# Weighted sum of two expert outputs: the order of three small transfers on ScalarE's queue

## The chip, the cores and the metric

The kernel runs on one core of a Trainium2 chip. The metric is the device time of the kernel in microseconds (us), the median of several runs. Its work is done by VectorE (DVE in the profile) and ScalarE (ACT); SyncE (SP) issues DMAs, and so does ScalarE. Sixteen DMA engines move the data between the chip's main memory (DRAM) and the on-chip buffer, which has 128 partitions.

## The reference

```python
def setup_inputs():
    batch, seq, hidden, n_experts, k = 16, 1024, 512, 8, 2
    return {
        "expert_outputs": np.random.randn(batch, seq, k, hidden).astype(np.float32),
        "combine_weights": np.random.randn(batch, seq, k).astype(np.float32),
    }

def reference(expert_outputs, combine_weights):
    weights = combine_weights[..., np.newaxis]
    return np.sum(expert_outputs * weights, axis=2).astype(np.float32)
```

For each of 16 x 1024 = 16,384 tokens, two rows of 512 numbers are multiplied by a weight each and added. 67 MB are read and 34 MB written.

## The kernel before

The 16,384 tokens are laid over 128 partitions, 128 tokens (`per`) on each. The last 13 (`LAST`) of each partition are a block of their own in DRAM, so the tokens of a partition are `main` = 115 and then 13. The 128 tokens are cut into ten tiles (`TILES`) of 12 or 13 tokens a partition. A tile has about 6.5 MB of input, and the on-chip buffer `et` has four rooms (`ROOM`), so the first four tiles are loaded at the start and a later tile is loaded into a room once the store of what was in it is done.

**Loads** are issued by SP (`load`, L76). The first four tiles take five loads (`FIRST`): 2 tokens a partition (1024 KB, cut to rows of 4,096 bytes), 11 (5632 KB, one row of 45,056 bytes a partition), 13, 12 and 13. They are called the first to the fifth load here. The first tile is the first and the second load together.

**Work on a tile** (`combine`): for eight of the ten tiles VectorE multiplies the whole tile by the broadcast weights (L88) and adds the halves (L97). In one tile ScalarE does part of the multiplying (L92 beside L94 and L96), and the last tile goes token by token through ScalarE and VectorE (L102, L103).

**Stores** (L130) are issued by ScalarE's queue, the last two by SP's.

**The weights** lie in `wt`, with the view `wk`. They come in three transfers on ScalarE's queue: the main weights, for the first 115 tokens of each partition (`weights(nc.scalar, 0, main)`, issued at L79; 128 rows of 920 bytes), and the last weights, for the other 13, in two halves of 64 partitions (L114; rows of 104 bytes).

**The zeroes**: VectorE fills `zt`, 16 x 128, with zeroes (L108), and one transfer (L111) writes them to 16 places of the output, 512 bytes at each, at the head of each sixteenth of the main block. The stores later write these places again, so the first store waits for the zeroes to land. The result does not depend on them.

The order on each engine is the order of the program text (`tc.manual_schedule()`). The built program hands out eight completion counters to the DMAs, in turn, in the order of the text. The ninth DMA of the text is the fifth load, and it has the counter of the first one; SP therefore waits, before it issues the fifth load, until the DMA that comes first in the text has landed.

Of the kernel before, what the change touches and what calls it, by code (L numbers as in the profile page):

```python
# [1 line left out]

# [4 lines left out]


@with_exitstack
def kernel(  # L10
    ctx: ExitStack,
    tc: tile.TileContext,
    expert_outputs: bass.AP,
    combine_weights: bass.AP,
    out: bass.AP,
):

    nc = tc.nc
    b, s, k, h = expert_outputs.shape
    assert k == 2
    n = b * s
    P = nc.NUM_PARTITIONS
    per = n // P
    assert per * P == n

    ROOM = [13, 13, 12, 13]
    ROOMS = len(ROOM)  # L30
    SITE = [sum(ROOM[:i]) for i in range(ROOMS)]
    TILES = [13, 13, 12, 13, 13, 13, 12, 13, 13, 13]
    FIRST = [2, 11, 13, 12, 13]
    STORES = [[0], [1], [2], [3], [4], [5], [6], [7, 8], [9]]
    WHOLE = [0, 1, 2, 3, 4, 5, 6, 7]
    MIXED = [8]
    ALONE = 3
    FREE = {9: 0}
    LAST = 13
    assert all(c <= ROOM[g % ROOMS] for g, c in enumerate(TILES))  # L40
    assert sum(TILES) == per and [g for st in STORES for g in st] == list(range(len(TILES)))
    main = per - LAST
    starts = [sum(TILES[:g]) for g in range(len(TILES))]

    def rows(x):

        first = x[0 : P * main, :].rearrange("(p t) f -> p t f", p=P)
        second = x[P * main : n, :].rearrange("(p t) f -> p t f", p=P)
        return lambda t, c: first[:, t : t + c, :] if t < main else second[:, t - main : t - main + c, :]

    flat = out.rearrange("b s h -> (b s) h")
    eo = rows(expert_outputs.rearrange("b s k h -> (b s) (k h)"))
    cw = rows(combine_weights.rearrange("b s k -> (b s) k"))
    o = rows(flat)

    dt = mybir.dt.float32
    mult = mybir.AluOpType.mult
    add = mybir.AluOpType.add
    copy = mybir.ActivationFunctionType.Copy

    pool = ctx.enter_context(tc.tile_pool(name="all", bufs=1))
    et = pool.tile([P, sum(ROOM), k * h], dt)
    halves = et.rearrange("p j (k h) -> p (j k) h", k=k)
    wt = pool.tile([P, per * k], dt)
    wk = wt.rearrange("p (t k) -> p t k", k=k)
    zt = pool.tile([16, 128], dt)
    warm = pool.tile([P, 1], dt)

    def place(t):
        g = max(g for g in range(len(TILES)) if starts[g] <= t)  # L70
        return SITE[g % ROOMS] + t - starts[g]

    def load(t, c, **kw):
        at = place(t)
        assert place(t + c - 1) == at + c - 1
        nc.sync.dma_start(out=et[:, at : at + c], in_=eo(t, c), **kw)  # L76

    def weights(q, t, c):
        q.dma_start(out=wk[:, t : t + c, :], in_=cw(t, c))  # L79

    def combine(g, base):
        at, c, t0 = SITE[g % ROOMS], TILES[g], starts[g]
        if g in WHOLE or g in MIXED:
            room = halves[:, k * at : k * (at + c), :]
            x0, x1 = et[:, at : at + c, 0:h], et[:, at : at + c, h : 2 * h]
            if g in WHOLE:
                wb = wt[:, k * t0 : k * (t0 + c)].unsqueeze(2).to_broadcast([P, k * c, h])
                nc.vector.tensor_tensor(out=room, in0=room, in1=wb, op=mult)  # L88
            else:
                for i in range(ALONE, c):  # L90
                    x = et[:, at + i, 0:h]
                    nc.scalar.activation(out=x, in_=x, func=copy, scale=wt[:, k * (t0 + i) : k * (t0 + i) + 1])  # L92
                w1 = wk[:, t0 : t0 + c, 1:2].to_broadcast([P, c, h])
                nc.vector.tensor_tensor(out=x1, in0=x1, in1=w1, op=mult)  # L94
                w0 = wk[:, t0 : t0 + ALONE, 0:1].to_broadcast([P, ALONE, h])
                nc.vector.tensor_tensor(out=x0[:, 0:ALONE], in0=x0[:, 0:ALONE], in1=w0, op=mult)  # L96
            nc.vector.tensor_tensor(out=halves[:, base : base + c, :], in0=x0, in1=x1, op=add)  # L97
            return
        for i in range(c):
            t = k * (t0 + i)  # L100
            x0, x1 = halves[:, k * (at + i), :], halves[:, k * (at + i) + 1, :]
            nc.scalar.activation(out=x0, in_=x0, func=copy, scale=wt[:, t : t + 1])  # L102
            nc.vector.scalar_tensor_tensor(  # L103
                out=halves[:, base + i, :], in0=x1, scalar=wt[:, t + 1 : t + 2], in1=x0, op0=mult, op1=add
            )

    with tc.manual_schedule():
        nc.vector.memset(zt, 0.0)  # L108

        ahead = flat[0 : P * main, :].rearrange("(q t) h -> q (t h)", q=16)  # L110
        nc.scalar.dma_start(out=ahead[:, 0:128], in_=zt)  # L111
        weights(nc.scalar, 0, main)
        for half in (slice(0, P // 2), slice(P // 2, P)):
            nc.scalar.dma_start(out=wk[half, main:per, :], in_=cw(main, per - main)[half])  # L114
        nc.scalar.activation(out=warm, in_=nc.const_aps.tensor(1.0, (P, 1), dt), func=copy)  # L115

        t = 0
        for i, c in enumerate(FIRST):
            load(t, c, **({"max_dma_last_dim": k * h * 4} if i == 0 else {}))
            t += c  # L120
        assert t == sum(TILES[:ROOMS])
        for j, st in enumerate(STORES):
            room = FREE.get(st[0], st[0] % ROOMS)
            base, c = SITE[room] * k, 0
            for g in st:
                combine(g, base + c)
                c += TILES[g]
            assert c <= k * ROOM[room]
            q = nc.sync if j in (7, 8) else nc.scalar
            q.dma_start(out=o(starts[st[0]], c), in_=halves[:, base : base + c, :])  # L130
            for g in st:
                if g + ROOMS < len(TILES):
                    load(starts[g + ROOMS], TILES[g + ROOMS])


# [1 line left out]
_INS = ['expert_outputs', 'combine_weights']  # L137
_OUTS = [((16, 1024, 512), 'float32')]


# [23 lines left out]
```

## Time and profile before

| | |
|---|---|
| time, median of 3 runs | 238.95 us (238.85 to 239.05) |
| span of the profiled execution | 237.1 us |
| outside the span, by the median | 1.85 us |
| VectorE busy | 190.0 us (80%) |
| ScalarE busy | 15.8 us (7%) |
| moved by DMA | 100.80 MB, mean 425 GB/s |

The span is that of one execution, taken by the hardware profiler, from the first instruction to the last. The times were taken without it, and the difference is taken as the same for both kernels. In the profile's rows L76 is line 76 of the kernel; SPq and ACTq are the queues of SP and ScalarE; `x <- y` gives what is written and what is read, or who waited for whom. q1 is the DMA queue that SP issues to, q10 that of ScalarE.

### The profile page before, as it was taken

The numbers are of one execution on the slowest core, as the hardware profiler recorded it, in microseconds if no ns is written. First come the engines' busy times: TensorE is split into PE (matmuls) and PEld (weight loads), VectorE is DVE, ScalarE is ACT, GpSimd is POOL, SyncE is SP. The second block draws the span as 40 slices with busy tenths as digits, with TensorE's granted clock in tenths as the row PEclk, the third lists the DMA queues.
The fourth block names the chain that finished last, engine by engine and source line by source line (L and its number), as shares of the span: only waits on it lengthen the run. The fifth ranks groups of instructions, "written<-read, shape, count | busy, mean of one in ns | idle before, by whom it ended". The sixth has DMA issues, their size and how long they took to land.

```text
span 237.1 us, 154 instructions
## 1 busy us (share of the span) xinstructions
DVE 190.0 (80%) x33; ACT 15.8 (7%) x25; POOL 0.2 (0%) x4
## 2 busy tenths in 40 slices
DVE  0006999999999999999999998998499969919400
ACT  2000000000000000000000000000000055019200
POOL 0000000000000000000000000000000000000000
DMA  8999999989999999999899999999899999899996
GB/s 300 388 481 434 432 421 398 470 348 485 449 431 458 431 440 390 486 420 420 359 492 409 409 509 392 431 503 431 359 431 503 420 397 483 381 431 431 431 431 287
DMA packets 3344, 100.80 MB, mean 425 GB/s; under 512 B 512, under 2 KB 656, under 8 KB 912
## 3 DMA queue, kind: packets, MB, share of 16 engines
q1 hardware_dynamic: 2000, 77.33, 75.9%
q10 hardware_dynamic: 1344, 23.47, 23.0%
HBM read 67.24 MB, written 33.56 MB: 425 GB/s over the span
## 4 chain that ended last, share of the span: by engine, by line
DVE 55%; DMA 36%; issue 1%; ACT 0%; DVEq 0%; ACTq 0%; SPq 0%
DVE et L88 35%; DVE et L97 17%; DMA out_dram<-et 17%; DMA et<-in_expert_outputs_dram 12%; DMA wt<-in_combine_weights_dram 8%; DVE et L103 3%; ACT et L102 0%; DVEq L159 0%; ACTq L111 0%; DVE zt L108 0%; DVEq L88 0%; SPq L76 0%; ACTq L102 0%
## 5 line engine op out<-in xcount | busy, mean ns | idle before, releaser
L88 DVE TENSOR_TENSOR et<-et,wt 128x13312 f32<-128x13312 f32 (+1 forms) x8 | 110.0, 13754 | 23.8 <-DMA wt<-in_combine_weights_dram 18.7
L97 DVE TENSOR_TENSOR et<-et 128x6656 f32<-128x6656 f32 (+1 forms) x9 | 62.8, 6973 | 0.4
L92 ACT ACTIVATE et<-et,wt 128x512 f32<-128x512 f32 x10 | 6.2, 708 | 188.0 <-DMA et<-in_expert_outputs_dram 188.0
L103 DVE SCALAR_TENSOR_TENSOR et<-et,wt 128x512 f32<-128x512 f32 x13 | 8.7, 747 | 5.0 <-ACT et L102 5.0
L102 ACT ACTIVATE et<-et,wt 128x512 f32<-128x512 f32 x13 | 8.1, 707 | 14.0 <-DMA et<-in_expert_outputs_dram 14.0
L94 DVE TENSOR_TENSOR et<-et,wt 128x6656 f32<-128x6656 f32 x1 | 7.1, 7093 | 2.3 <-DMA et<-in_expert_outputs_dram 2.3
L96 DVE TENSOR_TENSOR et<-et,wt 128x1536 f32<-128x1536 f32 x1 | 1.8, 1751 | 0.0
L115 ACT ACT_TABLE_LOAD x1 | 1.3, 1283 | 3.1 <-issue 3.1
L108 DVE MEMSET zt<- 16x128 f32 x1 | 0.2, 165 | 0.8 <-PEq L148 0.8
L115 ACT ACTIVATE warm<-const-float32-1.0 128x1 f32<-128x1 f32 x1 | 0.2, 203 | 0.0
L148 POOL MEMSET const-bfloat16-1.0<- 128x1 bf16 x1 | 0.1, 102 | 0.0
L148 POOL MEMSET const-uint8-127<- 128x1 uint8 x1 | 0.1, 101 | 0.0
L148 POOL MEMSET const-float32-0.0<- 128x1 f32 x1 | 0.1, 99 | 0.2 <-issue 0.2
L148 POOL MEMSET const-float32-1.0<- 128x1 f32 x1 | 0.1, 98 | 0.0
## 6 DMA issues: line engine op xcount, KB each, us to landing
et<-in_expert_outputs_dram SPq DMA_DIRECT2D x7, 6656.0 KB, 32.2
out_dram<-et ACTq DMA_DIRECT2D x5, 3328.0 KB, 34.7
et<-in_expert_outputs_dram SPq DMA_DIRECT2D x2, 6144.0 KB, 41.1
out_dram<-et SPq DMA_DIRECT2D x1, 6656.0 KB, 19.9
out_dram<-et ACTq DMA_DIRECT2D x2, 3072.0 KB, 37.2
et<-in_expert_outputs_dram SPq DMA_DIRECT2D x1, 5632.0 KB, 18.2
out_dram<-et SPq DMA_DIRECT2D x1, 3328.0 KB, 14.0
et<-in_expert_outputs_dram SPq DMA_DIRECT2D x1, 1024.0 KB, 5.0
```

The lines of the kernel that those rows point to most:

```text
L88: nc.vector.tensor_tensor(out=room, in0=room, in1=wb, op=mult)
L92: nc.scalar.activation(out=x, in_=x, func=copy, scale=wt[:, k * (t0 + i) : k * (t0 + i) + 1])
L94: nc.vector.tensor_tensor(out=x1, in0=x1, in1=w1, op=mult)
L96: nc.vector.tensor_tensor(out=x0[:, 0:ALONE], in0=x0[:, 0:ALONE], in1=w0, op=mult)
L97: nc.vector.tensor_tensor(out=halves[:, base : base + c, :], in0=x0, in1=x1, op=add)
L102: nc.scalar.activation(out=x0, in_=x0, func=copy, scale=wt[:, t : t + 1])
L103: nc.vector.scalar_tensor_tensor(out=halves[:, base + i, :], in0=x1, scalar=wt[:, t + 1 : t + 2], in1=x0, op0=mult, op1=add)
L108: nc.vector.memset(zt, 0.0)
L115: nc.scalar.activation(out=warm, in_=nc.const_aps.tensor(1.0, (P, 1), dt), func=copy)
L148: nc = _bacc.Bacc("TRN2", target_bir_lowering=False, num_devices=1)
```

## The change

ScalarE's queue issues the main weights first, then the zeroes, then the two halves of the last weights. Before, it was the zeroes, the main weights, the two halves. Nothing is added or taken away.

```diff
     with tc.manual_schedule():
         nc.vector.memset(zt, 0.0)
 
+        weights(nc.scalar, 0, main)
         ahead = flat[0 : P * main, :].rearrange("(q t) h -> q (t h)", q=16)
         nc.scalar.dma_start(out=ahead[:, 0:128], in_=zt)
-        weights(nc.scalar, 0, main)
         for half in (slice(0, P // 2), slice(P // 2, P)):
             nc.scalar.dma_start(out=wk[half, main:per, :], in_=cw(main, per - main)[half])
```

In the built program three more things differ. The zeroes are the second DMA of the text and have the second counter, and the main weights have the first. The fifth load thus waits for the main weights to land, where it waited for the zeroes. The first multiply (L88) and the first store (L130) wait for the same transfers as before, under the other counters.

## The prediction

> **What bounds the kernel now.** I read the page's slices and queues first, since this kernel does little but move bytes.
>
> ```profile
> span 237.1 us, 154 instructions
> DVE 190.0 (80%) x33; ACT 15.8 (7%) x25; POOL 0.2 (0%) x4
> ...
> DMA  8999999989999999999899999999899999899996
> ...
> DMA packets 3344, 100.80 MB, mean 425 GB/s; under 512 B 512, under 2 KB 656, under 8 KB 912
> ...
> q1 hardware_dynamic: 2000, 77.33, 75.9%
> q10 hardware_dynamic: 1344, 23.47, 23.0%
> ```
>
> VectorE is busy 80% of the span, but the two queues (q1 is SP's, q10 ScalarE's) keep the 16 DMA engines busy for 75.9 + 23.0 = 98.9% of it. Next I cut the span into stretches, to see whether the engines ever run dry. The columns are the stretch, its length, the busy time of DVE, ACT and POOL, the clock, the DMA share and GB/s. A packet counts where it starts, so a share can pass 1.
>
> ```profile
> 0.00:1.80 1.80, 0.17 (x1) 0.00 (x0) 0.20 (x4) 1.00 0.00 0
> 1.80:2.80 1.00, 0.00 (x0) 0.00 (x0) 0.00 (x0) 1.00 0.98 131
> 2.80:4.00 1.20, 0.00 (x0) 0.91 (x1) 0.00 (x0) 1.00 0.96 386
> ...
> 20.00:60.00 40.00, 39.93 (x4) 0.00 (x0) 0.00 (x0) 1.00 1.02 435
> 60.00:100.00 40.00, 39.93 (x5) 0.00 (x0) 0.00 (x0) 1.00 0.98 423
> 100.00:145.00 45.00, 44.52 (x5) 0.00 (x0) 0.00 (x0) 1.00 1.01 436
> 145.00:184.00 39.00, 34.31 (x4) 0.00 (x0) 0.00 (x0) 1.00 1.02 441
> 184.00:213.00 29.00, 22.18 (x4) 6.43 (x11) 0.00 (x0) 1.00 1.00 432
> ```
>
> From 2.8 us on the DMA share is about 1 in every stretch, at 423 to 441 GB/s. So from there the end is set by bytes, and the change moves no byte in or out. Only the first 2.8 us have room: nothing for 1.8 us, then 1 us with busy engines that move only 131 GB/s. The chain of waits tells another story, and I hold it against this one:
>
> ```profile
> 1.01 0.39 ACTq L111
> 1.40 0.03 issue
> 1.43 18.21 DMA wt<-in_combine_weights_dram
> ...
> 19.73 14.04 DVE et L88
> ...
> 33.78 7.09 DVE et L97
> ```
>
> By the chain the main weights, issued at 1.43 and landed at 1.43 + 18.21 = 19.64, release the first multiply (L88) at 19.73. The 20:60 and 60:100 rows above then show VectorE busy 39.93 of 40 us in both, so the chain says that an earlier start is worth having. The DMA shares say that VectorE and the DMA engines are both full there, and that the bytes decide the end. I go by the bytes.
>
> The three timed runs have a median of 238.95, which is 1.85 over the profiled span. I keep that 1.85 and sum against 237.1.
>
> **Part 1: the zeroes' memset no longer stands ahead of the main weights.** These are the issues at the start (start, length), then the transfers by size in KB and median us from issue to landing:
>
> ```profile
> 0.73 0.44 SPq L76 DMA_DIRECT2D et<-in_expert_outputs_dram  x1
> 1.01 0.39 ACTq L111 DMA_DIRECT2D out_dram<-zt  x1
> 1.22 0.46 SPq L76 DMA_DIRECT2D et<-in_expert_outputs_dram  x1
> ...
> et<-in_expert_outputs_dram SPq DMA_DIRECT2D x1, 5632.0 KB, 18.2
> et<-in_expert_outputs_dram SPq DMA_DIRECT2D x1, 1024.0 KB, 5.0
> out_dram<-zt ACTq DMA_DIRECT2D x1, 8.0 KB, 3.9
> ```
>
> The zeroes wait for the memset on VectorE (L108) and are issued at 1.01. The weights wait for nothing, so they can be issued about when SP issues its first load, 0.73: that is 1.43 - 0.73 = 0.7 us earlier. They are worth more than 0.7 at the landing, because of what they queue beside:
>
> ```profile
> q1 hardware_dynamic: 133, 0.54, 51.8%
> ...
> q10 hardware_dynamic: 32, 0.01, 2.8%
> ...
> q1 hardware_dynamic: 144, 5.90, 101.7%
> q10 hardware_dynamic: 144, 0.12, 2.6%
> ...
> q10 hardware_dynamic: 80, 0.01, 0.6%
> ```
>
> The first row is the stretch 0:3.9, in which q1 alone moved packets (133). The second is 3.9:5.2: q10's 32 are the zeroes, 16 packets and 16 completions. The next two are 6.6:20, where 144 packets of q1 stand against 144 of q10 (the 128 weight rows and 16 completions): they take turns, one for one, and each weight row waits out a 45,056-byte row of the second load. On an engine that is (20 - 6.6) / 8 = 1.7 us for each of its 8 weight rows, and this is why 115 KB need 18 us. The last row is 20:30, the last weights (64 of their 128 rows there).
>
> If the weights take the place of the zeroes, their first rows come at about 4 us, while the first load still has 256 - 133 = 123 rows of 4 KB to go, near 8 on each engine. The weights' 8 rows for each engine take turns with these, and land at 5 to 6 us; if two or three of them slip behind into the second load, each costs 1.7 us, and the landing is at about 10. Either way it is ahead of the second load, issued at 1.22 and landed 18.2 later, at 19.42. That load then releases the multiply. The gain at the multiply is at most 19.64 - 19.42 = 0.22 us, less what the zeroes and the last weights now put in front of the second load's end: 0.7 + 0.6 = under 1.3% of stretches of 5 to 10 us, some 0.1 us (taking half of the 2.8% of 1.3 us for the zeroes gives 0.02, twice the 0.6% of 10 us for the last weights gives 0.12). So VectorE starts some 0.1 us earlier. By the shares of about 1 from 20 us on, that is worth nothing at the end; if this cover were gone and VectorE alone set the end, it would be worth that 0.1.
>
> **Part 2: the zeroes move behind the weights, on ScalarE's queue alone.** Their 16 rows then land with or soon after the main weights, at 6 to 21 us instead of 1.01 + 3.9 = 4.9. They move past no other queue, but two waits follow them. The first store (L130) rewrites those places, so it waits for them; it is issued when the first sum is done, and the first multiply and sum need 14.04 and 7.09 us from 19.73, so at about 40.9. The other wait is SP's, for the fifth load:
>
> ```profile
> SPq L76 <- DMA out_dram<-zt: 2.1, 1, 2.1
> ...
> 4.92 0.33 SPq L76 DMA_DIRECT2D et<-in_expert_outputs_dram  x1
> ...
> et<-in_expert_outputs_dram SPq DMA_DIRECT2D x1, 6144.0 KB, 50.9
> ```
>
> The fifth load shares a completion counter with whatever ScalarE issues first. Now it waits 2.1 us for the zeroes and goes at 4.92. After the change it waits for the main weights, so it goes at 6 to 10, at the worst at 19.6. Queued behind it on SP is the sixth load, which needs a finished store anyway. SP's ring holds the fourth load (6144 KB) until over 50 us, so the fifth has over 30 us of slack. I cost this at nothing; the cover is those three loads already in the ring, and if they had landed by 19.6, each us of wait would be a us of idle DMA.
>
> **Part 3: two queues issue at once at the start.** This is the only term that can move the end.
>
> ```profile
> L76 SPq DMA_DIRECT2D et<-in_expert_outputs_dram x11: 327/328/643, 0.7 to 183.9; - x11
> ```
>
> An issue of SP's takes 328 ns alone, and up to 643 at the start where ScalarE issues beside it (0.44 and 0.46 above). In the kernel before SP's first issue has 1.01 - 0.73 = 0.28 us to itself; after, it hasn't. The bound above is 0.643 - 0.328 = +0.32 us on the first load. The bound below: weight rows that run while the engines only move 131 GB/s cost nothing there, and are gone from the full stretch later, 2.6% of 13.4 us = -0.35. I take 0, the middle, since nothing says which is nearer.
>
> A third price is between: if SP's first issue has to wait until ScalarE's is through, it loses one such issue, by the zeroes' row 0.39 us, and the time is 239.3 to 239.4. The bound from 0.643 speaks for something like it. By the Trainium skill (Perfetto Trace Analysis, DMA Instruction — HWDGE) the generator of DMA descriptors is shared by issuing queues and locked for exclusive use while it works for one, which would make that the price whenever ScalarE comes first; the trace, where the issues of both queues lengthen beside each other but overlap, agrees only in part.
>
> **The sum:** 237.1 + 0 (bytes) + 0 (start of VectorE, covered) + 0 (fifth load, covered) + 0 (-0.35 to +0.32, the start) + 1.85 = 238.95, say 239.0, with a range of its own of 238.6 to 239.3. A measurement of this kernel tells no change from about 0.2%, 0.48 us, so this is "same".
>
> **Rivals.**
> - *Slower: the weights get in front of the first load.* The zeroes came second, 0.28 after the load's issue, and showed no packet before 3.9, over 2.9 us after their own issue at 1.01; the first load's packets began 1.8 - 0.73 = 1.07 after its issue. So being second cost at least 1.8 us behind 256 rows. If the weights win the race at 0.73, the first load is second behind 128 rows: half of that, 0.9 us, in which the weights' own 0.35 us of work gets done: +0.55 to +0.9, 239.5 to 239.85, I say 239.6. If the 1 us of 131 GB/s repeats for the first load as well, it is +1.0. It decides as soon as ScalarE's first issue starts no later than SP's. For it: both would start at about 0.73, and the weights are a simpler pattern. Against it: the load may still go first, and then its packets run on as before.
> - *Faster: the chain is right.* The weight rows fall into the slow start, so the second load, no longer taking turns with them, lands 0.35 us earlier, at 19.07. VectorE then starts 19.64 - 19.07 = 0.57 earlier and, being busy 39.93 of 40, carries it to the end: 238.4. Against it: the weights' first rows may come as late as the zeroes', at 4 us, when the engines are already full.
> - *The change doesn't do what it says.* The weights' first rows still come after 5 us and take turns with the second load; they land near 19.5, the zeroes and the fifth load go behind them, and the time stays at 239.0.
>
> **The numbers.** The forecast has 0.40, the change without effect 0.08, the wait for one whole issue (239.3 to 239.4) 0.06; all three are "same", 0.54. The slower rival has 0.31, the faster one 0.15. The point is the likeliest case, 239.0. The range takes in the faster rival's 238.4 and the slower one's 239.85: 238.4 to 239.9.
>
> **What would show it.** In the changed profile the main weights should land at 5 to 10 us, and the idle time ahead of the first multiply should name the second load, ending at 19.5 to 19.7. SP's wait for the zeroes should be one for the main weights. The rows from 2.8 us on should keep a share of 1. The slower rival shows as a first load that lands later than 0.73 + 5.0, with few GB/s between 1.8 and 4; the faster one as a multiply that starts by 19.2 with a span shorter by as much. I am wrong if the engines run dry anywhere after 5 us, or if the end moves by more than the first 5 us do.

## The result, and the profile after

The changed kernel takes 239.5 us (median of 22 runs, 238.83 to 241.06), the kernel before 238.9 (22 runs, 238.83 to 240.95). The ratio is 1.0021, with a 95% interval of 1.0012 to 1.0031: slower by about 0.2%, 0.6 us by the medians. More telling than the median is the spread. Most runs of the kernel before lie within 0.3 us. Those of the changed kernel fall into groups: four at 238.83 to 238.90, as before, four at 239.05 to 239.15, eleven at 239.45 to 239.73, three at 240.0 and above.

The profiled run took 238.84, so it belongs to the first group and shows no loss. Span and queues, of the page after:

```profile
span 237.1 us, 154 instructions
...
q1 hardware_dynamic: 2000, 77.33, 75.7%
q10 hardware_dynamic: 1344, 23.47, 23.2%
```

The issues at the start of the changed kernel, from its timeline:

```profile
0.73 0.43 ACTq L79 DMA_DIRECT2D wt<-in_combine_weights_dram  x1
0.73 0.44 SPq L76 DMA_DIRECT2D et<-in_expert_outputs_dram  x1
```

Both queues issue at 0.73, as foretold. The transfers (KB, us from issue to landing):

```profile
et<-in_expert_outputs_dram SPq DMA_DIRECT2D x1, 5632.0 KB, 18.2
et<-in_expert_outputs_dram SPq DMA_DIRECT2D x1, 1024.0 KB, 5.3
wt<-in_combine_weights_dram ACTq DMA_DIRECT2D x1, 115.0 KB, 3.4
...
out_dram<-zt ACTq DMA_DIRECT2D x1, 8.0 KB, 6.4
```

The main weights land at 0.73 + 3.4 = 4.1 us instead of 19.64. The first load takes 5.3 instead of 5.0. The chain of waits and SP's waits:

```profile
1.22 18.22 DMA et<-in_expert_outputs_dram
...
19.57 14.04 DVE et L88
...
144.46 39.34 DMA out_dram<-et
```

```profile
SPq L76 <- DMA et<-in_expert_outputs_dram: 3.2, 1, 3.2
```

The second load has taken the weights' place ahead of the first multiply, which starts at 19.57 instead of 19.73. The last of these lines corrects a statement made ahead of the result: the fifth load does not wait for the main weights here but for the first load (3.2 us, then issued at 6.07). In the built program it is the first load that has the same counter as the fifth, and not the transfer that comes first in the text.

### The profile page after: what moved, and what is told of

It is laid out like the page before. It is cut to its first block, busy times and chain, and to the rows that moved or that the text cites. A ratio compares the mean times of both kernels' runs of the same rounds, so it can differ in the third digit from the quotient of the medians.

```text
span 237.1 us, 154 instructions
## 1 busy us (share of the span) xinstructions
DVE 190.0 (80%) x33; ACT 15.8 (7%) x25; POOL 0.2 (0%) x4
## 4 chain that ended last, share of the span: by engine, by line
DVE 55%; DMA 36%; issue 1%; ACT 0%; DVEq 0%; SPq 0%; ACTq 0%
DVE et L88 35%; DMA et<-in_expert_outputs_dram 20%; DVE et L97 17%; DMA out_dram<-et 17%; DVE et L103 3%; ACT et L102 0%; DVEq L159 0%; SPq L76 0%; DVEq L88 0%; ACTq L102 0%
## 5 line engine op out<-in xcount | busy, mean ns | idle before, releaser
L88 DVE TENSOR_TENSOR et<-et,wt 128x13312 f32<-128x13312 f32 (+1 forms) x8 | 110.0, 13754 | 23.7 <-DMA et<-in_expert_outputs_dram 23.7
L115 ACT ACTIVATE warm<-const-float32-1.0 128x1 f32<-128x1 f32 x1 | 0.2, 204 | 0.0
```

## The experiments

The times of the kernel before on the same chips were 238.87 to 238.88 (medians).

**The changed kernel again.** No edit; the aim is a profile of a run that lost time.

> The changed kernel once more, unaltered. Its 22 runs lay at 238.83 to 241.06 with a median of 239.5, and the one that was profiled took 238.84, so the profile in hand shows a run without the loss. Theory A (a race: both queues issue at 0.73, and the loss comes from how the two sets of descriptors fall at the start): the times spread again over more than 0.5, from 238.8 up, and a profile of a run above 239.3 shows the loss inside the first 20 us, as a first or second load that lands 0.3 to 1 us later. Theory B (a fixed cost of small weight rows ahead of the first load): the times gather near one value, 239.5. Theory C (the order that is set up at the start is carried on, and the time goes later, where a store and a load take turns): the first 20 us look alike, and a row of the DMA share well below 1 stands somewhere after 20 us.

239.49 (11 runs, 238.81 to 239.74), ratio 1.0021 (1.0012 to 1.0030). The profiled run took 239.37. Two more runs were profiled, with these expectations:

> The changed kernel once more, for one more profile beside the two in hand. In the one of 238.84, ScalarE's queue (q10) moved 86 packets in the first 2.8 us and SP's (q1) 23; in the one of 239.37 it was 5 against 32. Theory A: the two go together. With over 50 packets of q10 in the first 2.8 us the time is 238.8 to 239.1; with under 20 it is 239.3 to 239.8, and the first load's landing is over 5.5 us from its issue. Theory B (weight rows ahead cost): the other way round. No link: either count with either time.

> As for the run before: the changed kernel, a fourth profile, and the same link of packet count and time by theory A (over 50 packets of q10 by 2.8 us with 238.8 to 239.1, under 20 with 239.3 to 239.8).

They took 238.85 and 239.52. So there are four profiles of one program, two without the loss and two with it. What each queue moved in the first 2.8 us (packets, MB, share) tells them apart. First the run of 238.84, then that of 238.85:

```profile
q10 hardware_dynamic: 86, 0.08, 19.2%
q1 hardware_dynamic: 23, 0.09, 13.4%
```

```profile
q10 hardware_dynamic: 97, 0.09, 18.0%
q1 hardware_dynamic: 31, 0.13, 17.7%
```

And the two that lost time, of 239.37 and of 239.52:

```profile
q1 hardware_dynamic: 32, 0.13, 33.6%
q10 hardware_dynamic: 5, 0.00, 0.6%
```

```profile
q1 hardware_dynamic: 41, 0.17, 31.9%
q10 hardware_dynamic: 14, 0.01, 1.4%
```

In the runs without loss most of the 128 weight rows go in the slow first us. In the others the first load's rows go first, and most of the weight rows come among them after 2.8 us. In all four the first issues of the two queues start within 0.01 us of each other, so these do not show what decides. Theory A's link was drawn from the first two profiles; the other two bear it out.

Where the time goes can be read from the loads' landings. First and fourth load of the run of 239.52, then of the run of 238.85 (the fourth is issued at about 2.2 in both):

```profile
et<-in_expert_outputs_dram SPq DMA_DIRECT2D x1, 1024.0 KB, 5.6
...
et<-in_expert_outputs_dram SPq DMA_DIRECT2D x1, 6144.0 KB, 51.3
```

```profile
et<-in_expert_outputs_dram SPq DMA_DIRECT2D x1, 1024.0 KB, 5.2
...
et<-in_expert_outputs_dram SPq DMA_DIRECT2D x1, 6144.0 KB, 50.8
```

The first load lands 0.4 us later and the fourth, at 53 us, 0.5; the difference at the end is 0.67. A landing is that of the slowest of 16 DMA engines, and the packet records show that it is the slowest that fell back: in the run of 239.37 the third load lands on the 16 engines from 34.84 to 35.51 us, in the kernel before from 34.85 to 35.24. The first engine is as early, the last 0.27 later. These are the packets that start after 235 us, for the runs of 238.84, 239.37 and 239.52 (16 of them are the last store's completions):

```profile
DMA packets 16, 0.00 MB, mean 0 GB/s; under 512 B 16, under 2 KB 16, under 8 KB 16
```

```profile
DMA packets 23, 0.19 MB, mean 37 GB/s; under 512 B 16, under 2 KB 16, under 8 KB 16
```

```profile
DMA packets 27, 0.29 MB, mean 59 GB/s; under 512 B 16, under 2 KB 16, under 8 KB 16
```

In the runs with the loss 7 and 11 rows have yet to start, in the run without it none. A second part is lost near 43 us, where the first store starts: the rows of the fourth load that go just ahead of the store's own first rows last 2.0 to 2.7 us instead of 1.8, mostly one on each engine, in the run of 239.52 two. All that the rows last longer from 40 to 56 us, shared over the 16 engines, is the second column here. The other columns are times in us: when the engines start on the fourth load, and when their last rows end (the mean of the 16, and the slowest). The records do not name the engine, so the 16 rows of the fourth load that start first and the 16 rows that end last stand for one engine each.

| run | fourth load, mean | slowed rows, per engine | end, mean | end, slowest |
|---|---|---|---|---|
| kernel before | 34.59 | 0.44 | 235.77 | 235.98 |
| 238.84 | 34.50 | 0.50 | 235.72 | 235.89 |
| 238.85 | 34.41 | 0.54 | 235.68 | 235.89 |
| 239.37 | 34.67 | 0.62 | 236.01 | 236.40 |
| 239.52 | 34.54 | 0.87 | 236.14 | 236.59 |

In each row the mean end is the sum of the first two columns and 200.72 to 200.74 us, so nothing else makes the mean engine late. The slowest engine then ends 0.17 to 0.21 us behind the mean without the loss, and 0.39 and 0.45 with it. The loss has these two parts: slowed rows (0.18 and 0.43 us more than in the kernel before) and engines out of step (0.18 and 0.24 more). The engines are out of step within the first 20 us, where theory A looked; the slowed rows come later, where theory C looked, though the DMA share does not fall well below 1 there. Why the slowed rows cost more was not found.

**Behind the first load, for certain.**

```diff
         nc.vector.memset(zt, 0.0)
+        nc.vector.memset(wt[:, 0:1], 0.0)
         weights(nc.scalar, 0, main)
```

> The main weights still come first and the zeroes second, but VectorE first writes one column of the weights' tile, so that the weights are issued at about 1.05 and SP's first load always goes ahead by 0.3 us. Theory A: no race, so the spread shrinks to that of the kernel before (0.3) and the median goes to 238.8 to 239.0. Theory B: the weight rows come behind the first load, so 238.9 as well, with the same small spread. Theory C, or a cost of the late zeroes or of the fifth load's wait for the weights: 239.3 to 239.7, as in the changed kernel.

238.88 (11 runs, ten of them 238.81 to 238.99), ratio 0.9999 (0.9990 to 1.0007). Its issues' landings:

```profile
et<-in_expert_outputs_dram SPq DMA_DIRECT2D x1, 1024.0 KB, 5.2
...
wt<-in_combine_weights_dram ACTq DMA_DIRECT2D x1, 115.0 KB, 8.3
```

The order of the three transfers is that of the change, the weights land at 1.02 + 8.3 = 9.3 us, and the zeroes come late, but ten of the eleven runs show no loss; the eleventh took 239.56. So neither the order on ScalarE's queue nor the late zeroes cost the time; it goes with the issue beside SP's first load.

**Ahead of the first load, for certain.** SP's first load waits instead:

```diff
         nc.vector.memset(zt, 0.0)
+        nc.vector.memset(et[:, 0:1, 0:1], 0.0)
         weights(nc.scalar, 0, main)
```

> The changed kernel, with VectorE first writing one element of the place of the first load, so that SP's first load is issued at about 1.05 and the weights always go ahead by 0.3 us. The other loads are issued later by that too. Theory A: no race, so a small spread; the time is that of the changed kernel's best runs plus at most the 0.3 that the load is late, 238.8 to 239.2. Theory B: the weight rows always hold up the first load, 239.5 to 239.9, small spread. Theory C: 239.3 to 239.7 with a spread of over 0.5.

239.03 (11 runs, 238.80 to 241.01), ratio 1.0018 (1.0000 to 1.0035). Seven runs lie at 238.80 to 239.04, four above 239.3. The profiled run (238.99) has all the weights through by 2.8 us:

```profile
q1 hardware_dynamic: 18, 0.07, 20.8%
q10 hardware_dynamic: 144, 0.12, 16.1%
```

The median is in A's range, the spread is not. Weight rows that are issued first are mostly free, not always. The race is thus not the whole of it.

This profile also sets the two parts of the loss against each other. The engines are as far out of step as in the run of 239.52: they start on the second load from 5.22 to 5.89 us here, from 5.19 to 5.87 there. But the rows at the first store cost only 0.42 us an engine, as in the kernel before, and the last row ends at 236.04, 0.06 later than in that kernel. After 235 us one row has yet to start:

```profile
DMA packets 17, 0.03 MB, mean 5 GB/s; under 512 B 16, under 2 KB 16, under 8 KB 16
```

So engines out of step at the start are not enough for the loss.

**Both on one queue.** SP issues the weights, then its loads:

```diff
-        weights(nc.scalar, 0, main)
...
+        weights(nc.sync, 0, main)
         t = 0
         for i, c in enumerate(FIRST):
```

> The main weights are issued by SP, ahead of its first load, instead of by ScalarE; ScalarE issues the zeroes at 1.01 and the last weights. One queue holds both, so nothing decides their order by chance, and the weight rows run in the slow start. The first load is issued at about 1.17. Theory A: a small spread, 238.7 to 239.2 (the load 0.44 later, less the 0.35 of weight rows that the slow start hides). Theory B: the rows ahead of the first load cost 0.5 to 0.9, 239.4 to 239.8.

240.29 (10 runs, 238.97 to 241.34), ratio 1.0051 (1.0027 to 1.0075). Both theories missed: it is slower than B's 239.8 and spreads most. In its profile (241.11) the weights land 2.0 us after their issue, but the packet records show engines apart by 1.1 us from the first load on and, from the first store's landing, by 2.3. No race between the weights and the first load is left here, so A does not explain it. Five of the ten runs lie near 241. Such runs are not particular to this kernel: the changed kernel has one (241.06), and the kernel before has one in 22 (240.95).

**Same moment, few rows.** The kernel before, with SP's first load held until the zeroes' issue:

```diff
         nc.vector.memset(zt, 0.0)
+        nc.vector.memset(et[:, 0:1, 0:1], 0.0)
```

> The kernel before (zeroes, main weights, last weights), with VectorE first writing one element of the place of the first load, so that SP's first load waits until about 1.03 and is issued beside the zeroes, which go at about 1.01. Two queues issue at the same moment, but ScalarE's transfer has 16 rows instead of 128. Theory A1 (issuing at the same moment is enough): the kernel before plus up to 0.3 for the late load, plus 0.3 to 0.6 in many runs, 239.3 to 239.8 with a spread of over 0.5. Theory A2 (it takes the 128 weight rows among the first load's): 238.9 to 239.2, with a small spread.

```profile
1.01 0.45 ACTq L112 DMA_DIRECT2D out_dram<-zt  x1
1.03 0.96 SPq L76 DMA_DIRECT2D et<-in_expert_outputs_dram  x2
```

239.16 (12 runs, ten at 239.08 to 239.20, one each at 239.45 and 241.12), ratio 1.0011 (1.0002 to 1.0020). The load is 1.03 - 0.73 = 0.30 us late and the time 0.29 longer, with a small spread in the ten. Issuing at the same moment does nothing by itself with 16 rows. It also suggests that a delay of the first load is paid in full when little else runs in its place; with the weight rows in its place, above, the same delay cost 0.16 by the median. The profile is of the run of 241.12: in it one engine's last row ends 1.9 us after that of the next engine, and in the run of 241.11 above two engines end 1.7 and 0.9 behind the others. Here no weight row starts by 2.8 us, so rows of the weights that come early are not needed for a run near 241.

**Half of the last weights in front.**

```diff
+        nc.scalar.dma_start(out=wk[0 : P // 2, main:per, :], in_=cw(main, per - main)[0 : P // 2])
         nc.scalar.dma_start(out=ahead[:, 0:128], in_=zt)
         weights(nc.scalar, 0, main)
-        for half in (slice(0, P // 2), slice(P // 2, P)):
-            nc.scalar.dma_start(out=wk[half, main:per, :], in_=cw(main, per - main)[half])
+        nc.scalar.dma_start(out=wk[P // 2 : P, main:per, :], in_=cw(main, per - main)[P // 2 : P])
```

> The kernel before, with one half of the last weights (64 rows of 104 bytes) moved to the head of ScalarE's queue: half, zeroes, main weights, other half. So ScalarE issues a small transfer at 0.73, beside SP's first load, while the main weights stay behind the zeroes; the fifth load waits for that half. Theory A1 (any issue of ScalarE's beside SP's first one upsets the start): 239.2 to 239.6 and a spread of over 0.5. Theory A2 (it takes the 128 weight rows beside the first load's rows): 238.8 to 239.0, spread as before. Under both the wait of the fifth load costs nothing.

239.49 (8 runs, 239.40 to 239.83), ratio 1.0025 (1.0015 to 1.0035). This seems to speak for A1, but not by its reason: there is nearly no spread, and the engines reach the second load at 4.85 to 5.26 us, earlier than in the kernel before (5.00 to 5.33). What differs is that the main weights land later and VectorE starts at 23.37. The rows at the first store then cost 1.1 us on each engine instead of 0.44. So another experiment moved VectorE's start alone.

**VectorE late.**

```diff
+            if g == 0:
+                late = et[:, at + 2 : at + 5, :]
+                nc.vector.tensor_tensor(out=late, in0=late, in1=late, op=mybir.AluOpType.max)
             if g in WHOLE:
```

> The kernel before, with one more operation on VectorE ahead of the first multiply: the maximum of three tokens' rows with themselves (128x3072), which changes nothing and takes some 3.2 us. All transfers at the start stay as they are. If VectorE's start is covered by the full DMA engines: 238.8 to 239.1. If the loss of the kernel with the half in front (239.49, where VectorE started 3.6 us late and the rows beside the first store were slowed 1.1 us on each engine instead of 0.4) came from the later first store: 239.3 to 239.7, with those rows slowed as much. If the chain of waits holds: 242.

240.41 (5 runs, 240.30 to 240.52), ratio 1.0065 (1.0052 to 1.0077). No theory gave this. From its timeline and stretches:

```profile
19.29 3.36 DVE L88 TENSOR_TENSOR et<-et 128x3072 f32<-128x3072 f32 x1 [18.31 <-DMA et<-in_expert_outputs_dram]
22.68 14.02 DVE L91 TENSOR_TENSOR et<-et,wt 128x13312 f32<-128x13312 f32 x1
```

```profile
20.00:60.00 40.00, 39.90 (x5) 0.00 (x0) 0.00 (x0) 1.00 1.01 421
60.00:100.00 40.00, 39.93 (x5) 0.00 (x0) 0.00 (x0) 1.00 1.01 436
100.00:145.00 45.00, 44.93 (x5) 0.00 (x0) 0.00 (x0) 1.00 0.99 430
```

```profile
DMA packets 33, 0.45 MB, mean 91 GB/s; under 512 B 16, under 2 KB 16, under 8 KB 16
```

The first multiply starts 22.68 - 19.73 = 2.95 us later and the end comes 1.5 later. The DMA share stays at 1, but 20 to 60 us moves 421 GB/s instead of 435: full engines move less. The records give 1.2 us an engine for slowed rows from 44 to 52 us, 0.8 more than before, and the rest is mostly one engine, which ends 1.0 us behind the next (by the last line, 17 rows start after 235 us). So a VectorE that starts later, and with it a later first store, does cost time, though the engines are not idle.

Over the other profiles the cost of the slowed rows does not simply grow with VectorE's start: it is 0.37 to 0.54 us for starts at 19.51 to 19.76 us and 0.60 to 0.87 at 19.80 to 20.28, but 0.62 and 0.67 at 19.34 and 19.44. In the two runs of the changed kernel with the loss VectorE starts at 19.90 and 19.80, so its start may be what slows their rows more; no run moves it alone by so little, and this is not shown.

**ScalarE's activation ahead of the weights.** `weights(nc.scalar, 0, main)` moved behind the activation (L115).

> The kernel before, with ScalarE's first activation and its table load moved ahead of the main weights, which are thus issued near 3 to 4.6 instead of 1.43. They take turns with the second load later and land at 21 to 25 instead of 19.64, so that VectorE starts 1.5 to 5 us later. If the bytes set the end (the DMA engines stay full, and VectorE's start is covered): 238.8 to 239.1. If the chain of waits sets it: later by as much as VectorE starts later, 240.4 to 244.

```profile
1.43 1.28 ACT L112 ACT_TABLE_LOAD   x1 [1.43 <-DVE zt L108]
1.50 0.38 ACTq L79 DMA_DIRECT2D wt<-in_combine_weights_dram  x1
```

238.85 (11 runs, 238.83 to 238.92), ratio 0.9997 (0.9988 to 1.0006). The edit did not do what it was meant to: the issue does not wait for the table load before it, goes at 1.50, and the weights aren't late. It is a kernel like the one before with a smaller spread, and is the same in time; no kernel tried beats the one before.

**Without the zeroes.** L112 left out of the changed kernel, and then of the one whose weights wait for the memset:

> The changed kernel without the transfer of the zeroes; the weights are issued at 0.73 and the fifth load waits for them, as in the changed kernel. Theories A and B: the zeroes have no part in it, so 239.3 to 239.7 and (A) the spread of over 0.5 stay. If the late zeroes cost the time (each of the 16 engines takes them at another place in the row of the second load's rows), 238.8 to 239.0 and a small spread.

> The kernel in which the weights wait for VectorE's memset and go 0.3 us behind the first load (238.88, as the kernel before), now without the transfer of the zeroes. The changed kernel without the zeroes took 239.69, 0.2 more than with them, and in its trace a row that is slowed beside the first store comes twice. If the zeroes save the first store that second slow row: 239.05 to 239.3 here. If their absence only mattered through the race at the start: 238.8 to 239.0.

239.69 (6 runs, 239.47 to 239.84), ratio 1.0030 (1.0019 to 1.0042), and 238.94 (12 runs, 238.84 to 241.02), ratio 1.0017 (0.9999 to 1.0036). The late zeroes are not the cause: without them the changed kernel is no faster. In the first one's profile (239.72) the weight rows came among the first load's (8 of q10's packets by 2.8 us), as in the lossy runs. In the second, eight of twelve runs are at 238.84 to 239.01, so the zeroes are hardly worth anything in most runs; two runs near 241 carry its wide interval. The other four lie at 239.14 to 241.02, against one late run in eleven with the zeroes, which these few runs cannot tell apart. So weights issued 0.3 us behind the load do not rule out such runs.

## Why the prediction was right or wrong

**The point.** 239.0 was forecast with 238.4 to 239.9; measured 239.5, inside the range. The likeliest case, no change within 0.2%, was missed narrowly: the ratio of 1.0021 is at the bound and its interval excludes 1. The time is near the 239.6 of the slower rival, whose mechanism did not happen. That the range held it is thus in part luck: the range was stretched for that rival.

**The term that was mis-sized** is part 3, "two queues issue at once at the start", taken as 0 between -0.35 and +0.32. In the four profiles it was about 0 (238.84, 238.85) and +0.5 and +0.65 (239.37, 239.52) over 238.87, above the upper bound. That bound came from how long an issue lasts, and the issues hardly lengthened: side by side SP's lasted 0.44, as before, and ScalarE's 0.43, against 0.38 where it was issued 0.30 ahead of SP's. So a lock of the descriptor generator while it works for one queue, as the Trainium skill has it (Perfetto Trace Analysis, DMA Instruction — HWDGE), is not seen in these rows as a wait of one queue for the other's issue.

What moved was two things that the sum did not have. It took the 16 engines as one pipe, and the kernel ends with the slowest, which fell 0.18 and 0.24 us further behind the mean. And it took full engines to mean a fixed time for the bytes, but the rows at the first store lasted 0.18 and 0.43 us an engine longer. The prediction's own sign of being wrong, "if the end moves by more than the first 5 us do", shows this in the run of 239.52: the mean engine comes to the fourth load at 34.54 us, no later than the 34.59 of the kernel before, and ends 0.37 later.

**The slower rival** had the right size and the wrong sign of its mechanism. It said that the time is lost if the weights get in front of the first load. In the profiles of the changed kernel they got in front where nothing was lost, and the loss came where the load's rows went first. Its price for a late first load agrees in kind with the held load beside the zeroes, 0.29 for 0.30 us.

**The faster rival** failed at its last step. In the run of 238.84 the weight rows did fall into the slow start (171 GB/s from 1.8 to 2.8 us against 131), but the multiply started 0.16 earlier, not 0.57, and nothing came of it.

**The weights' landing**, 5 to 10 us, was 4.0 to 5.4 in the profiles. **VectorE's start**, "some 0.1 us earlier", was 0.16 to 0.22 earlier in the runs without loss and 0.1 to 0.2 later in the others. That an earlier start is worth nothing holds: the kernel with the weights at 1.50 started at 19.44, as the runs without loss near 19.5, with the time of before. The reason given, that full engines decide the end, held only that way round. "If this cover were gone ... it would be worth that 0.1" had no price for a start that is later under full engines, and that is half: 1.5 us for 2.95. **The fifth load**: costed at nothing, rightly; it went at 6.07, though behind another transfer than was said. Where it did wait for the main weights, in the kernel that issues them at 1.02, it went at 9.35 and the time was that of before.

**Shown and open.** Shown: in the four profiles of the changed kernel the loss goes with which queue's rows come first, and it consists of slowed rows at the first store and of engines out of step; it goes from ten of eleven runs when the weights follow 0.3 us behind the load; it does not come from the order on the queue, the zeroes, or two issues at one moment as such. Open: what picks the winner when the first issues agree to 0.01 us, why weight rows among or ahead of the first load put the engines out of step (the kernel with both on SP's queue has it without a race), why the rows at the first store are slowed by such different amounts, and what makes the runs near 241, which the kernel before has too.

## What to carry to other kernels

In a kernel whose DMA engines are never idle, the end is that of the slowest of the 16 engines, and engines that count as busy need not move bytes at a fixed rate. So ask of a change at the start whether it keeps the engines in step and what it shifts later on, and not only how many bytes it moves. Here a small transfer was better issued 0.3 us behind a big first load than beside it, even though it then landed later, since it still landed before it was needed. When repeated runs of a changed kernel spread and those before do not, one profile shows one case only; take several and look for what differs between those that lost time and those that did not.

## What the runs showed of the hardware

Two queues that issue within 0.01 us of each other gave two different orders of rows (86 to 97 against 5 to 14 packets of one queue by 2.8 us) from one program. In the kernel before and the four profiles of the changed one, the load rows just ahead of the first store's own rows last 2.0 to 2.7 us instead of 1.8, mostly one on each engine, from near 43 us on, and in the kernel before no such rise is seen at the later stores; DMA time is lost there while the engines count as busy (0.44 us an engine in the kernel before, 1.1 and 1.2 where the store starts 3 to 4 us later). And ScalarE issued a DMA at 1.50 us, behind a table load that began at 1.43 and takes 1.28: the issue did not wait for it.
